# A hybrid decoder step on one core: the opening pipelined by feature tile with products two tiles behind, cache copies moved, the attention's operations reordered

## The chip, the core and the metric

The kernel runs on one core of one Trainium2 chip. Its time is the device time of one execution in microseconds (us); the median of the runs is what is compared. Before the change three runs gave 1983.94, 1985.59 and 1988.86 us, median 1985.59. The core has a matrix engine (TensorE, PE in the profile, with its weight loads apart as PEld), a vector engine (DVE), a scalar engine (ACT), a general engine (GpSimd, POOL) and a queue engine (SyncE, SP), which here issues nearly all transfers. Each engine works through its own instructions in order; semaphores tie them together. All data is float32, and matrix products read it as fp32r, rounded by a cast.

## The reference, cut to what matters

One layer of a decoder trunk for a prompt of 2048 rows and 8 sample rows, of width 1024:

```
mod = c @ w_ada + b_ada;  shift, scale, gate = split(mod, 3)
h = rmsnorm(x, norm_g) * (1 + scale) + shift
z = h @ w_in      # columns: q 1024 | k 256 | v 256 | attention gate | rnn x | rnn gate | merge gates A, B
q, k = rmsnorm per head of 64, times q_g, k_g
o = band_attention(q, k, v)   # blocks of 128 rows over 256 keys, window 128, relative bias, a sink per head
ya = o * silu(ga)
yr = rglru(conv(xr)) * silu(gr)
y = x + gate * ((sigmoid(ma) * (ya @ w_pa) + sigmoid(mr) * (yr @ w_pr)) @ w_out)
```

The sample rows go through the same layer, with their attention over a window of 128 cached rows. The kernel also returns the moved window: rows 1 to 127 of each cache copied down by one row, and a new last row; the same for the convolution's state.

## The kernel before

The prompt is done in two halves of 1024 rows (`s` = 0 and 1). A value that enters a product is held as two fp32r tiles, a high part (an ACT cast) and the rest (a DVE subtraction); a product is three matmuls: high x high, high x low, low x high. This pair of operations is a "split".

**Opening** (lines 1923 to 2103), for the first half. It makes the modulation and h, 128 features (`f`, 8 tiles) at a time, and the k/v products of the first 512 rows on the way, in four PSUM banks `kvp`. For tile f: `mod_load` (286) loads two columns' blocks of `w_ada` (4 transfers of 256 KB); `mod_cols` (309) multiplies them by c on PE (`col_tiled`, 299: products, then an ACT copy of the result) and `mod_finish` (314: two PE transposes, four DVE operations); a DVE operation makes the scale `gsT`; `x_evac(0, f)` (1942) turns four 128x128 blocks of x on PE and `h_evac` (380) applies scale and shift on ACT and splits the result into `hT[f]`; then 24 matmuls multiply it with the k and v weights. From f = 4 on each step also turns two tiles of rows 512 to 1023 (`x_evac(1, ...)`). The x tiles, 128 rows each, are scaled row by row first (`rms_rows`, 365: two squares on ACT, three small operations on POOL, two on DVE). `h_evac` leaves a store of h to DRAM, which runs behind the loop (`late`, 2051). The copies of the caches and of the convolution's state are three DRAM to DRAM transfers issued on POOL's queue (2101 to 2103).

The order of the work is partly the planner's: the framework's scheduler orders instructions by their place in the program and by when it thinks them ready. Instructions issued while `pinned[0]` is set (line 48) keep the order of the program on their engine. In the opening `pinned` is not set; it is set in the attention.

**k/v phase** (`phase_kv`, 506): the remaining rows' k and v, norms, transposes and splits, with the relative bias table on the side. `skn`, the negated sinks, comes from a small load (2060 to 2063).

**Attention** (`phase_attn`, 558): 16 units (4 groups of heads x 4 pairs of row blocks) in a software pipeline over `i`: in one iteration the q product of unit i, the logits and softmax of unit i-1, and the output product of unit i-2. In order: `stage_b4` (softmax normalisation of i-2: DVE reciprocal, POOL multiplication, for each of two row blocks); `gemm_a` (191), the first half of the q product, 24 matmuls into one half of a PSUM bank; `stage_a1` (562) of that half: square on ACT, sum on DVE, power on POOL; `stage_b1`: four transposes of q on PE and its split; the second `gemm_a` into the other half of the same bank and its `stage_a1`; `stage_c1`: eight transposes of the softmax result, a copy on ACT and a masked copy on DVE for each block; `stage_b2`: 24 logit matmuls; `stage_b0`: a small copy on POOL; `stage_c2`: the output product; `stage_b3` of the first block (DVE minimum, ACT exponentials); `stage_a2` (q scaled by its norm on DVE); `stage_c3`; `stage_b3` of the second block. Splits of the next weights are spread over four places of the iteration by `weights` (786), which has due times for each half.

**Recurrent stage and projections** (`stages`, 1254): gates, convolution, recurrence, projections, as steps of 12 matmuls of 512 columns. `line.on(t, rank, fn)` hangs loads, splits and evacuations on step t; weights are loaded 7 steps and split 2 steps ahead.

Of the kernel before, what the change touches and what calls it, by code (L numbers as in the profile page):

```python
# [21 lines left out]
P = 128  # L22
# [19 lines left out]
def tile_hybrid_step(ctx: ExitStack, tc: tile.TileContext, x_prompt, x_sample, cache_k, cache_v, state_conv,  # L42
# [63 lines left out]
    def H(shape, dt=F32):  # L106
        return hp.tile([P] + shape, dt, tag="H", name=nm("H"))
# [73 lines left out]

    def load_half(rows, cols, pin=False):

        return split_raw(load_raw(half_srcs(rows, cols)), 256, pin)
# [373 lines left out]
    def phase_attn(s, hT, sa, kT, vt, chunks, line):  # L558
# [255 lines left out]
        for i in range(N + 2):  # L814
# [25 lines left out]
            if i < N:  # L840
                u, tp = seq[i]
                ps_[i], ss_[i] = PG(), M([8])
                gemm_a(ps_[i], wqs[u], hT, 2 * tp * P, 0)
                stage_a1(ps_[i], ss_[i], 0)
            elif i == N:
                fill(nh - 3)
            else:
                line.emit(0)
            if 1 <= i <= N:
                qk_[i - 1] = stage_b1(ub, tb, qn_.pop(i - 1))  # L850
            weights(2 * i, 1)
            slot(1)
            if i < N:
                if s == 1 and tp == 1:
                    next(smp[u])
                if pend:
                    next(pend.pop(0))
                gemm_a(ps_[i], wqs[u], hT, (2 * tp + 1) * P, 1)
                if pend:
                    next(pend.pop(0))  # L860
                if tp == 3:
                    drop(wqs.pop(u))
                if s == 1 and tp == 1:
                    next(smp[u])
                stage_a1(ps_[i], ss_[i], 1)
            elif i == N:
                fill(nh - 2)
            else:
                line.emit(1)
            weights(2 * i + 1, 0)  # L870
            if 2 <= i:
                t2 = seq[i - 2][1]
                c_[i - 2] = [stage_c1(2 * t2 + t, lt) for t, lt in enumerate(lt_.pop(i - 2))]
                c_[i - 2] = [fn() for fn in c_[i - 2]]
            slot(2)
            if i == N + 1:
                line.emit(2)
            if 1 <= i <= N:
                lps = stage_b2(ub, tb, *qk_.pop(i - 1))
                lts = [stage_b0(ub) for _ in range(2)]  # L880
            if 2 <= i:
                u2, t2 = seq[i - 2]
                po = stage_c2(u2, c_.pop(i - 2))
                if u2 == 3:
                    free(vt[1][t2])
            if 1 <= i <= N:
                sm_[i - 1] = [stage_b3(ub, 2 * tb, lps[0], lts[0])]
# [15 lines left out]
            weights(2 * i + 1, 1)  # L903
# [350 lines left out]
    def stages(s, hT, hT1=None, side=None):  # L1254
# [682 lines left out]

    def kv_load():
        w = w_in[0][len(wkv) * 512:(len(wkv) + 1) * 512]
        wkv.append([load_half(w, [(OFF_K, 256)], True), load_half(w, [(OFF_V, 256)], True)])  # L1940

    def x_evac(g, f):
# [3 lines left out]
        h_evac(0, ps, 512, f, g * 512, hT)  # L1946
        if f == KT - 1:
            free(*xts[4 * g:4 * g + 4])

# [41 lines left out]

    ada_load()
    vrows_first()
# [3 lines left out]
    for xt in xts:  # L1997
        rms_rows([xt[:, 0:512], xt[:, 512:1024]], P)
    ada_load()
    kv_load()  # L2000
    x_load(1)
    ada_load()
    x_load(1)
# [13 lines left out]
    for f in range(KT):  # L2017
        if f < 2:
            ada_load()
            x_load(1)  # L2020
        elif len(ada) < KT:
            if f == 2:
                kv_load()
            ada_load()
        if f < 4:
            xt = xts[4 + f]
            rms_rows([xt[:, 0:512], xt[:, 512:1024]], P)
        if f == 4:
            next(rest)
        if f in (5, 6):  # L2030
            next(table)
        mod_cols([8 + f, f], ada[f], PQ, PT)
        V.tensor_scalar(gsT[:, f, :], modT[:, 8 + f, :], 1.0, VT[:, 24 + f:25 + f], op0=ALU.add, op1=ALU.mult)
        hT.append([S([2, 512], F32R) for _ in range(2)])
        x_evac(0, f)
        xh, xl = col(hT, f, 0, 512)
        for tt in range(4):
# [8 lines left out]
        if f >= 4:  # L2046
            x_evac(1, 2 * (f - 4))
            x_evac(1, 2 * (f - 4) + 1)
    next(rest)
    bias_load()  # L2050
# [49 lines left out]

    for dst, src in ((k_win_s[0, :, 0:127], cache_k[0, :, 1:128]), (v_win_s[0, :, 0:127], cache_v[0, :, 1:128]),
                     (conv_s[0, :, 0:2], state_conv[0, :, 1:3])):
        tc.keep_in_program_order(G_.dma_start(dst, src))
# [41 lines left out]
```

## Time and profile before

| | |
|---|---|
| median of three runs | 1985.59 us (1983.94 to 1988.86) |
| the profiled execution | 1991.77 us, its span 1990.1 us |
| PE busy | 1930.7 us (97%) |
| DVE, ACT, POOL busy | 1375.0, 988.4, 409.4 us |
| mean granted PE clock | 0.995 of full speed |
| moved by DMA | 286.62 MB |

The profile is of one execution. Busy time counts instructions that compute; the ends of matmuls are modelled. A "wait" is idle time of an engine ahead of an instruction and the engine that released it. In the timeline a row is one instruction or several merged ones: start, duration, engine, operation, output and inputs by tile name, shapes, count, and in brackets the idle time before it. The tiles: B and S are the large SBUF buffers, H and M small ones, pg, pq and pt the PSUM banks. Nearly all rows have the line L60, that of the wrapper that issues them, so tile names tell them apart.

### The profile page before, as it was taken

How to read it: one execution, taken by the hardware profiler on the slowest of the kernel's cores; microseconds unless marked ns; L12 is line 12 of the kernel's file. 1: busy time of each engine (PE TensorE's matmuls, PEld its weight loads, DVE VectorE, ACT ScalarE, POOL GpSimd, SP SyncE). 2: the span in 40 equal slices, each digit the busy share in tenths (PEclk: the TensorE clock that was granted, in tenths of full speed). 3: DMA queues.
4: the chain of work that ended last, by engine and by line, in shares of the span. 5: the costliest groups of instructions: out<-in, count | busy, mean ns of one | idle time of the engine just before them, and what ended most of it. 6: DMA issues, size and time to landing. Idle time of an engine off the chain costs nothing. (4 is left out here: it accounts for less than half of the span.)

```text
span 1990.1 us, 32504 instructions
## 1 busy us (share of the span) xinstructions
PE 1930.7 (97%) x11504; PEld 1571.9 (79%) x11504; DVE 1375.0 (69%) x2894; ACT 988.4 (50%) x2199; POOL 409.4 (21%) x540
## 2 busy tenths in 40 slices
PE   6899999999999999999999999999999999999999
PEld 4788887778888878887898888777887877777777
DVE  3447777766878885578744766677677879754965
ACT  4335555435665766514423555543465757542221
POOL 4113443000201112152012344310011111111600
PEclk9999999999999999999999999999999999999999
DMA  9520214552433457986622121445233334458673
GB/s 304 178 75 12 86 49 148 151 183 87 150 98 113 143 180 226 321 296 191 224 60 57 36 62 49 143 130 153 78 118 100 127 102 164 141 174 291 219 230 111
DMA packets 307688, 286.62 MB, mean 144 GB/s; under 512 B 57073, under 2 KB 224229, under 8 KB 307486
## 3 DMA queue, kind: packets, MB, share of 16 engines
q1 hardware_dynamic: 307398, 282.41, 45.3%
q8 instruction: 90, 1.47, 0.3%
q0 software_dynamic: 128, 2.15, 0.3%
q14 instruction: 72, 0.59, 0.1%
HBM read 200.69 MB, written 85.93 MB: 144 GB/s over the span
## 5 line engine op out<-in xcount | busy, mean ns | idle before, releaser
L60 PE MATMUL pg<-S,B 128*128 128x512 f32 (+1 forms) x4224 | 1003.8, 392 | 4.2 <-DVE B L60 3.8
L60 PEld LDWEIGHTS pg<-S,B 128*128 128x128 f32 (+1 forms) x4224 | 773.5, 188 | 189.5 <-issue 11.9
L60 DVE TENSOR_TENSOR B<-B,B 128x512 fp32r<-128x512 f32 (+1 forms) x732 | 537.8, 757 | 157.7 <-ACT B L60 147.9
L60 PE MATMUL pq<-S,B 128*128 128x512 f32 (+2 forms) x1920 | 411.0, 378 | 5.9 <-DVE B L60 5.7
L60 PEld LDWEIGHTS pq<-S,B 128*128 128x128 f32 (+1 forms) x1920 | 316.3, 187 | 84.1 <-DVE B L60 9.7
L60 POOL TENSOR_TENSOR B<-B,B 128x512 f32<-128x512 f32 x128 | 191.3, 1511 | 926.3 <-DVE B L60 518.3
L60 ACT CAST B<-B 128x512 fp32r<-128x512 f32 x468 | 280.3, 617 | 111.2 <-DVE B L60 72.1
L60 PE MATMUL pg<-B,S 128*128 128x256 f32 x1872 | 249.0, 289 | 17.6 <-ACT H L60 12.8
L60 PEld LDWEIGHTS pg<-B,S 128*128 128x128 f32 x1872 | 231.9, 192 | 36.6 <-ACT H L60 19.8
L60 ACT CAST S<-B 128x512 fp32r<-128x512 f32 x184 | 108.8, 620 | 95.8 <-DVE B L60 40.3
L60 DVE TENSOR_TENSOR S<-B,S 128x512 fp32r<-128x512 f32 x184 | 143.2, 808 | 14.8 <-ACT S L60 14.6
L60 ACT ACTIVATE B<-B 128x512 f32<-128x512 f32 (+1 forms) x150 | 93.1, 630 | 116.4 <-DVE B L60 108.7
L60 ACT ACTIVATE B<-B,M 128x129 f32<-128x129 f32 x260 | 102.6, 396 | 72.1 <-DVE M L60 53.4
L60 POOL TENSOR_TENSOR B<-B,M 128x512 f32<-128x512 f32 x64 | 70.4, 1121 | 170.4 <-DVE M L60 170.4
L60 DVE SCALAR_TENSOR_TENSOR B<-B,pg 128x512 f32<-128x512 f32 x78 | 53.1, 682 | 74.8 <-PE pg L60 67.0
L60 POOL TENSOR_TENSOR M<-M,mhalf 128x4 f32<-128x4 f32 (+3 forms) x102 | 96.3, 944 | 8.5
L60 DVE TENSOR_TENSOR B<-pq,B 128x512 f32<-128x512 f32 x96 | 65.9, 686 | 44.1 <-PE pq L60 37.9
L60 ACT COPY B<-pg 128x512 f32<-128x512 f32 x80 | 46.9, 586 | 90.1 <-PE pg L60 81.7
L60 DVE TENSOR_REDUCE M<-H 128x4 f32<-128x256 f32 (+1 forms) x85 | 35.1, 414 | 80.3 <-ACT H L60 79.0
L60 ACT COPY H<-pt 128x256 f32<-128x256 f32 (+1 forms) x47 | 15.6, 333 | 150.1 <-PE pt L60 150.1
L60 DVE SCALAR_TENSOR_TENSOR B<-B,VT,B 128x512 f32<-128x512 f32 x96 | 81.1, 845 | 2.3
L60 DVE SCALAR_TENSOR_TENSOR B<-B,B 128x512 f32<-128x512 f32 x106 | 72.0, 684 | 0.4 <-ACT B L60 0.2
(201 smaller groups left out, 1711.5 us busy)
## 6 DMA issues: line engine op xcount, KB each, us to landing
B<-in_w_in_dram SPq DMA_DIRECT2D x144, 256.0 KB
B<-in_w_in_dram SPq DMA_DIRECT2D x128, 128.0 KB
B<-yad SPq DMA_DIRECT2D x56, 256.0 KB
B<-hd SPq DMA_DIRECT2D x48, 256.0 KB
B<-in_w_out_dram SPq DMA_DIRECT2D x48, 256.0 KB
S<-in_w_ada_dram SPq DMA_DIRECT2D x32, 256.0 KB
S<-in_x_prompt_dram SPq DMA_DIRECT2D x16, 512.0 KB
hd<-B SPq DMA_DIRECT2D x32, 256.0 KB
```

The costliest lines, as they stand in the source:

```text
L60: ins = fn(*args, **kw)
```

## The change

It has four parts, none of which changes what is computed.

- **Opening.** `pinned[0]` is set from the first load to the end of the loop, so that every engine keeps the program's order. The loop runs ten steps in place of eight: step f does the modulation product, the x turns, and the evacuation of tile f, and the k/v products of tile f-2, 12 matmuls before and 12 after `mod_finish`. The k/v weights are loaded early without being split, and split a quarter at a time at even steps (`kv_split`); loads stand in a table by step. The row scalings of x tiles 0 to 3 are in step 0, those of the others in steps 2, 4 and 5. The tiles of rows 512 to 1023 are turned in steps 7 to 9. `bias_load` moves into step 7.
- **Cache copies.** The three transfers leave the opening for steps 46, 60 and 74 of the first half's recurrent stage, still on POOL's queue.
- **q norm.** `stage_a1` squares the whole bank (512 wide) once, after both halves; `stage_a3` sums and takes the power of all 8 columns, behind `stage_c1`'s copies.
- **Order.** Weight splits are done at one place of an iteration, ahead of the second half; `stage_b4` does both blocks in one go; `stage_b0` comes ahead of `stage_c1`'s copies; a slot for steps of the next stage moves behind `stage_c2`.

```diff
-        def stage_a1(ps, ss, t):
-            sq = H([256])
-            A.activation(sq, ps[:, t * 256:(t + 1) * 256], AF.Square)
-            o = ss[:, 4 * t:4 * t + 4]
-            V.tensor_reduce(o, sq.rearrange("p (h d) -> p h d", d=HD), op=ALU.add, axis=AX.X)
-            rstd_of(o, o, 4, 1.0 / HD)
+        def stage_a1(ps):
+            sq = Tt([512])
+            A.activation(sq, ps, AF.Square)
+            return sq
+
+        def stage_a3(sq):
+            ss = M([8])
+            V.tensor_reduce(ss, sq.rearrange("p (h d) -> p h d", d=HD), op=ALU.add, axis=AX.X)
+            free(sq)
+            rstd_of(ss, ss, 8, 1.0 / HD)
+            return ss
...
-                lt_[i - 2] = [stage_b4(*sm_[i - 2][0])]
-            weights(2 * i, 0)
-            if 2 <= i:
-                lt_[i - 2].append(stage_b4(*sm_.pop(i - 2)[1]))
+                lt_[i - 2] = [stage_b4(*x) for x in sm_.pop(i - 2)]
...
                 gemm_a(ps_[i], wqs[u], hT, 2 * tp * P, 0)
-                stage_a1(ps_[i], ss_[i], 0)
...
-            weights(2 * i, 1)
+            weights(2 * i + 1, 1)
             slot(1)
...
-                stage_a1(ps_[i], ss_[i], 1)
+                sq = stage_a1(ps_[i])
...
-            weights(2 * i + 1, 0)
             if 2 <= i:
                 t2 = seq[i - 2][1]
                 c_[i - 2] = [stage_c1(2 * t2 + t, lt) for t, lt in enumerate(lt_.pop(i - 2))]
+            if 1 <= i <= N:
+                lts = [stage_b0(ub) for _ in range(2)]
+            if 2 <= i:
                 c_[i - 2] = [fn() for fn in c_[i - 2]]
-            slot(2)
+            if i < N:
+                ss_[i] = stage_a3(sq)
...
-            weights(2 * i + 1, 1)
...
+            for t, dst, src in ((46, k_win_s[0, :, 0:127], cache_k[0, :, 1:128]),
+                                (60, v_win_s[0, :, 0:127], cache_v[0, :, 1:128]),
+                                (74, conv_s[0, :, 0:2], state_conv[0, :, 1:3])):
+                line.on(t, LOAD, lambda dst=dst, src=src: G_.dma_start(dst, src))
...
+    pinned[0] = True
+    vrows_first()
     ada_load()
...
+    loads = ([lambda: x_load(1), ada_load], [ada_load, kv_load], [lambda: x_load(1), ada_load], [lambda: x_load(2)],
+             [ada_load], [ada_load], [], [], [], [])
...
+    for f in range(KT + 2):
+        for load in loads[f]:
+            load()
+        if f < KT:
+            mn = col_tiled(PT(), cT, ada[f][0], 256)
+            free(*ada[f][1])
+            if f == 0:
+                for i in range(4):
+                    x_rms(i)
+            xps = x_turn(0, f)
+        if f > 1:
+            kv_part(f - 2, (0, 1))
+        if f < KT:
+            mod_finish([8 + f, f], mn, PT)
+            V.tensor_scalar(gsT[:, f, :], modT[:, 8 + f, :], 1.0, VT[:, 24 + f:25 + f], op0=ALU.add, op1=ALU.mult)
+            hT.append([S([2, 512], F32R) for _ in range(2)])
+            x_evac(0, f, xps)
+        if f % 2 == 0 and f < KT:
+            kv_split(f // 4, f % 4 // 2)
+        for i in {7: (0,), 8: (2, 3), 9: (5, 6)}.get(f, ()):
+            second(i)
+        if f > 1:
+            kv_part(f - 2, (2, 3))
+        for i in {2: (4,), 4: (5,), 5: (6, 7)}.get(f, ()):
+            x_rms(i)
...
+        if f == 7:
+            bias_load()
+        for i in {7: (1,), 8: (4,), 9: (7,)}.get(f, ()):
+            second(i)
+    pinned[0] = False
```

More of the change, by code (lines that the diff above doesn't have):

```diff
@@ L879, in phase_attn @@
                 lps = stage_b2(ub, tb, *qk_.pop(i - 1))
-                lts = [stage_b0(ub) for _ in range(2)]
             if 2 <= i:
@@ L885, in phase_attn @@
                     free(vt[1][t2])
+            slot(2)
             if 1 <= i <= N:
@@ L1936, in ada_load, with kv_split, x_turn @@
         ada.append(mod_load([8 + f, f], S, 4))
+    kvr = []
     def kv_load():
-        w = w_in[0][len(wkv) * 512:(len(wkv) + 1) * 512]
-        wkv.append([load_half(w, [(OFF_K, 256)], True), load_half(w, [(OFF_V, 256)], True)])
-    def x_evac(g, f):
+        w = w_in[0][len(kvr) * 512:(len(kvr) + 1) * 512]
+        kvr.append([load_raw(half_srcs(w, [(c, 256)])) for c in (OFF_K, OFF_V)])
+    def kv_split(h, r):
+        if r == 0:
+            wkv.append([[], []])
+        for j in range(2):
+            wkv[h][j].extend(split_raw(kvr[h][j], 256, halves=(r,)))
+    def x_turn(g, f):
         ps = PT() if g else PQ()
@@ L2016, in tile_hybrid_step, with kv_part @@
     rest, table = vrows_rest(), bias_table()
[L2017 to L2035, printed above, removed]
+    def kv_part(f, tts):
         xh, xl = col(hT, f, 0, 512)
-        for tt in range(4):
+        for tt in tts:
             c = slice(tt * P, (tt + 1) * P)
```

30 lines of the change are left out of this document (13 added, 17 removed).

## The prediction, made before the change was run

> **What bounds the kernel now.** I read the page first.
>
> ```profile
> span 1990.1 us, 32504 instructions
> ```
> ```profile
> PE 1930.7 (97%) x11504; PEld 1571.9 (79%) x11504; DVE 1375.0 (69%) x2894; ACT 988.4 (50%) x2199; POOL 409.4 (21%) x540
> ```
>
> TensorE (PE) is the bound: only 1990.1 - 1930.7 = 59.4 us of the span has no matmul running. Work on another engine is worth something only where it makes PE wait or where PE's clock sinks. So the next view is the busy time by stretch, to see where PE is not full.
>
> ```profile
> 0.00:25.00 25.00, 12.33 (x64) 7.16 (x65) 8.24 (x25) 11.97 (x29) 14.07 (x56) 1.00 0.93 284
> 25.00:50.00 25.00, 19.02 (x164) 14.75 (x162) 10.66 (x35) 12.82 (x28) 6.99 (x24) 0.99 1.12 328
> 72.00:76.00 4.00, 4.00 (x21) 4.00 (x21) 0.73 (x5) 0.03 (x1) 0.00 (x0) 0.50 0.46 168
> 116.00:120.00 4.00, 3.24 (x18) 3.25 (x19) 2.17 (x5) 1.33 (x4) 1.20 (x2) 0.71 0.19 73
> 400.00:500.00 100.00, 100.00 (x452) 78.44 (x451) 64.69 (x118) 45.91 (x83) 0.00 (x0) 1.00 0.46 139
> ```
>
> The columns are the stretch, its length, busy time of PE, PE's weight loads, VectorE (DVE), ScalarE (ACT) and GpSimd (POOL), then granted clock, DMA share and GB/s. In the recurrent stages (last row) PE has no gap, so nothing can be won there. In the first 50 us it is busy 31.4 us, while the DMA engines are full (0.93, 1.12): the opening waits for loads. And the clock sinks twice, at 72 and at 116 us. For the rest I asked the waits, first of the matmuls, then of the weight loads.
>
> ```profile
> PE pg L60 <- ACT H L60: 12.8, 19, 1.8
> ```
> ```profile
> PEld pg L60 <- ACT H L60: 19.8, 28, 2.1
> ```
>
> The matmuls' largest wait is for ACT writing an "H" tile: 12.8 us in 19 waits. That tile is the square that `stage_a1` takes of half the q bank. The timeline of one attention iteration shows the mechanism.
>
> ```profile
> 207.01 3.10 PE L60 MATMUL pg<-B,S 128*128 128x256 f32 x24
> 209.95 0.60 PE L60 MATMUL pt<-ident,B 128*128 128x128 f32 x4
> 211.58 3.11 PE L60 MATMUL pg<-B,S 128*128 128x256 f32 x24 [1.04 <-ACT H L60]
> 214.52 1.04 PE L60 MATMUL pt<-ident,B 128*128 128x128 f32 x8
> ...
> 218.98 3.12 PE L60 MATMUL pg<-B,S 128*128 128x256 f32 x24
> ```
> ```profile
> 210.65 0.60 ACT L60 CAST B<-B 128x512 fp32r<-128x512 f32 x1
> 211.16 0.37 ACT L60 ACTIVATE H<-pg 128x256 f32<-128x256 f32 x1
> ```
> ```profile
> 212.21 2.49 POOL L60 TENSOR_TENSOR B<-B,M 128x512 f32<-128x512 f32 x2 [6.05 <-DVE M L60]
> ```
>
> The first half of the q product ends near 209.95. Its square should follow, but ACT still has exponentials and a weight cast (210.65) in its queue and squares only at 211.16. The second half writes the same bank, so PE waits for that read until 211.58. The POOL row is the softmax's normalisation, two tiles of 1.25 us, which the second set of transposes at 214.52 reads.
>
> **The change: attention.** It removes the half squares: `stage_a1` now squares the whole bank behind both halves, so the second half has no reader to wait for. All 28 such waits go. How much is that? Ends of matmuls are modelled; the transposes at 209.95 start about 0.12 us apart, so the next matmul could have started at 210.43, which makes the gap 1.15 us, not the 1.04 shown. The true sum lies between 12.8 (PE) and 19.8 (weight loads, which can stand early for other reasons); with 0.1 us more on most I take **14.5**.
>
> What comes late next? Let an iteration start with the first half at 0. From the starts above a half takes 2.94 us, the four transposes 0.5, the eight 0.97, and the logit and output products together 218.98 - 215.49 = 3.5, where 215.49 is 214.52 plus 0.97; PE alone needs 10.85 us where this iteration took 11.97. The second half ends at 6.4. The square on ACT costs one 512-wide activation (0.63, row below) in place of two 256-wide (0.37 each). `stage_c1`'s transposes end at 7.35, the copy and mask behind them on ACT and DVE at about 8.5, and the output product that reads them starts near 9: 0.5 us of slack. `stage_a3`'s reduction, queued on DVE behind these masks, ends near 9.2, and the power on POOL follows.
>
> ```profile
> L60 POOL TENSOR_TENSOR M<-M,mhalf 128x4 f32<-128x4 f32 x6 | 6.1, 1017 | 0.5
> ```
>
> The power of 8 columns isn't in the trace; it lies between one of 4 (1.02 us) and two (2.03). I take 1.6, nearer to two, since columns and not calls seem to be paid. So `stage_a2` is ready near 11.1 on DVE, just as DVE ends the first softmax part. If the power takes 2.03, the second softmax part behind it on DVE moves by 0.4 us, its exponentials too, and the multiplications on POOL for the next iteration's `stage_c1`. With softmax parts of some 2 us on DVE and 1.25 us for each multiplication, the same walk has those ready near 6.0 and wanted at 6.9; `stage_b4` now issues both reciprocals with no weight split between or ahead of them in its iteration, which helps. So 0.4 us is covered; without this cover it would cost up to 0.4 us in each of 32 iterations, 13 us, the far bound. Weight splits move to one place, between `stage_b1` and the second half; two of them together at three iterations of each sequence half are 1.2 us on ACT, under 2.94 us of matmuls, and cost nothing. I give 1 us back for new waits: **13.5** for this part, bounds 1.5 and 17 (0.15 us under each of the 28 early weight loads left out).
>
> The dip at 116 us follows the first of these waits. With 0.71 granted over 4 us it loses 0.29 x 4 = **1.2 us**, which goes with the wait; at worst nothing.
>
> **The change: opening.** Its rows are a step's modulation, turns and second transposes on PE, the stall, the last product, the loads (count, size), the issue of a small one, and ACT's operations (count, busy us, mean ns).
>
> ```profile
> 37.49 1.07 PE L60 MATMUL pq<-S,cT 128*32 128x256 f32 x16
> 38.49 0.65 PE L60 MATMUL pq<-ident,S 128*128 128x128 f32 x4
> 39.05 0.44 PE L60 MATMUL pt<-ident,H 128*128 128x128 f32 x2
> ```
> ```profile
> 69.23 0.18 DVE L60 TENSOR_SCALAR skn<-M 128x16 f32<-128x16 f32 x1 [5.46 <-DMA M<-in_sinks_dram]
> ```
> ```profile
> 70.65 2.93 PE L60 MATMUL pg<-B,S 128*128 128x256 f32 x12 [3.56 <-DVE S L60]
> ...
> 75.58 0.56 PE L60 MATMUL pq<-B,S 128*128 128x256 f32 x1
> ...
> 77.15 1.90 PE L60 MATMUL pq<-B,S 128*128 128x256 f32 x14
> ...
> 81.00 0.88 PE L60 MATMUL pt<-B,S 128*128 128x256 f32 x6
> ```
> ```profile
> q0 software_dynamic: 128, 2.15, 6.8%
> ...
> S<-in_w_ada_dram SPq DMA_DIRECT2D x32, 256.0 KB
> S<-in_x_prompt_dram SPq DMA_DIRECT2D x8, 512.0 KB
> hd<-B SPq DMA_DIRECT2D x16, 256.0 KB
> B<-in_w_in_dram SPq DMA_DIRECT2D x8, 256.0 KB
> ```
> ```profile
> 53.46 0.41 SPq L60 DMA_DIRECT2D H<-in_b_rg_a_dram  x1
> ```
> ```profile
> L60 ACT ACTIVATE B<-S 128x512 f32<-128x512 f32 x16 | 10.0, 628 | 8.7 <-DMA S<-in_x_prompt_dram 8.5
> L60 ACT CAST S<-B 128x512 fp32r<-128x512 f32 x16 | 9.5, 622 | 0.1
> L60 ACT ACTIVATE B<-pt,modT,gsT 128x512 f32<-128x512 f32 x8 | 6.2, 780 | 12.1 <-PE pt L60 12.1
> ```
>
> Now: the last k/v product of the opening ends at 81.9, with 18 products of the next stage ("pq", from 75.58 to 77.15) already done, 2.2 us at the 2.94/24 = 0.122 of the half above, so the opening is worth 79.7 us. Part of that is the stall at 70.65: DVE's in-order queue held `skn`, which waited for a small load, ahead of the split that PE needed (3.56 us), and the half clock at 72 behind it (0.5 x 4 = 2 us).
>
> After: the loads ahead of the last modulation tile are 8 + 4 + 2 MiB = 14.7 MB. The rows give 25 x 284 = 7.1 MB by 25 us and 328 GB/s from there, so it lands at 25 + 7.6/0.328 = 48.1 us. Before, the copies of the caches (2.15 MB, 6.6 us at that rate) ran in between; the change moves them out. The same sum lands tiles 3, 5 and 6 (7.9, 11.5, 13.6 MB) at 27.4, 38.4 and 44.8.
>
> PE needs per step f: 1.07 modulation, 0.65 turns, 0.44 its transposes, and 24 products of step f-2, 2.9: 5.1 us, less than the 6.5 between landings. But all is in program order now. PE's second transposes wait for ACT's copy (256 wide, as the square at 211.16: 0.37), which stands behind the previous step's evacuation (0.78 + 0.62), weight splits (two casts) and up to two tiles of squares (four of 0.63 and their reads, about 3.3). Walking both queues gives steps 3 to 7 at 28.8, 35.1, 40, 46.4 and 53 us: 5 us behind the loads at the end. From there PE has 1.07 + 0.65 + 0.44, three k/v steps (8.8) and eight turns (5.2), 16.2 us, filled by products two behind: end at 69.2. The gain is 79.7 - 69.2 = **10.5 us**. Bounds: 15.4 if the steps follow the landings (48.1 + 16.2), nothing if ACT's order eats it all.
>
> Moves that cost nothing: POOL's one-hot selections now stand ahead of the first row scaling, in time in which POOL has nothing else until the first x tile has been squared. On SP the nine small vector loads stand ahead of the last modulation load; SP issues ahead of the landings, which hides them, else it is 9 x 0.41 = 3.7 us. The stores of h (4 MiB) follow as a burst and end before the next stage's weights are wanted. The `skn` load is behind the pinned loop now; should its DVE instruction still slip in, 3.56 + 2 us come back. The three copies go on POOL's queue in the recurrent stage, where POOL does nothing (0.00) and the DMA share is 0.46; loads there are issued seven products of 12 matmuls ahead, 84 x 100/452 = 18.6 us, so a copy ahead of one costs nothing, or at worst a few us once.
>
> **Sum.** 10.5 + 13.5 + 1.2 = 25.2 us. The profiled execution took 1991.8 us (span 1990.1 and 1.7 around it), so 1966.6 there. The median of the runs, 1985.59, is 6.2 below it; the prediction is for that median: 1985.6 - 25.2 = **1960.4**.
>
> **The rivals.** (1) The opening pays nothing, because ACT's in-order copies and not the loads set the pace. For it: ACT is the fuller queue of a step with squares. Against: in the first 50 us it is busy 24.8. It leaves 14.7 us of gain: 1970.9. (2) The attention's wait is replaced: the output product waits for its masks, or `stage_c1` for POOL. For it: slacks of 0.5 and 0.9 us only. Against: no engine but PE is full. The opening alone gives 1985.6 - 10.5 - 1.2 = 1973.9. (3) Slower: PE's gaps in the load-bound opening put its clock at half, as after the 3.56 us at 67 us (0.50 at 72). At half clock a step costs 10.2 us, not 5.1: five steps from tile 2 at 24 us end at 75, and the 16.2 become 32.4, together 107, 28 us later than now; less 14.7 it gives 1998.6. It decides once the gap in each step passes about 3.5 us. Against: the first 50 us have 18.6 us of gaps and still a clock of 1.00 and 0.99. (4) No change: the scheduler already hides what is removed, 1985.6.
>
> The Trainium skill ("TensorE: Matmul & The Clock Gate", Part 1) has the rule behind (3): after an idle window of about 3.4 us the array gets half its clock until it has been busy as long. By that rule one long gap costs some 1.7 us and a gap of that length in every step gives rival 3. The trace agrees where PE stood 3.56 us; gaps of 1 to 2 us, which I expect, fall under the window.
>
> **How the numbers follow.** Chances: forecast 0.67, (1) 0.12, (2) 0.13, (3) 0.05, (4) 0.03. Forecast's own best: 15.4 + 17 + 1.2 = 33.6, or 1952; its weak side meets rival 2 at 1974. With a little for the runs' own spread the range is 1951 to 1976; only (3), (4) and part of the tails are outside. A change under 0.3% (6 us) can't be told from none here. Forecast, (1) and (2) are all faster by more: 0.92; same 0.03; slower 0.05.
>
> **What would show it.** Right: no wait of q products for ACT's squares; an iteration near 10.9 us; no DMA on the software queue before 100 us; the eighth modulation product at 49 to 53 us; no stall of PE for DVE near 67; the opening's last k/v product near 68 and the rest shifted by about 25 us. Wrong: waits of "pt" products for DVE or POOL in the attention, a clock near 0.5 over several opening stretches, a modulation product that waits for ACT, or gaps in the recurrent stage near the copies.

## The result, and the profile after

The changed kernel takes 1970.05 us (median of four runs, 1966.61 to 1970.6), the kernel before beside it 1984.94: a ratio of 0.9918, with a 95% interval from 0.9900 to 0.9936, 14.9 us. The prediction was 1960.4 in a range of 1951 to 1976. So the direction and the range were right, and of the 25.2 us that the sum promised 10 did not come. The measured time is the number of the prediction's rival 1 (1970.9), which the range also held. The two terms of the sum were not wrong alike: further down, the attention gives its 14.7 us and more, and the opening next to nothing.

The page of the changed kernel, whose profiled execution took 1970.57 us, and its stretches (the same columns as those shown of before):

```profile
span 1968.9 us, 32371 instructions
...
PE 1918.9 (97%) x11504; PEld 1569.0 (80%) x11504; DVE 1376.8 (70%) x2862; ACT 985.0 (50%) x2167; POOL 391.3 (20%) x476
```
```profile
0.00:25.00 25.00, 10.12 (x65) 4.38 (x67) 7.92 (x28) 9.81 (x23) 12.87 (x64) 1.00 0.93 281
25.00:50.00 25.00, 22.24 (x212) 17.67 (x209) 11.14 (x34) 14.66 (x32) 2.18 (x8) 1.00 0.95 274
72.00:76.00 4.00, 4.00 (x35) 4.00 (x35) 3.12 (x13) 2.12 (x6) 0.20 (x1) 1.00 0.66 225
116.00:120.00 4.00, 4.00 (x19) 3.25 (x18) 1.85 (x4) 0.60 (x1) 2.12 (x4) 1.00 0.00 0
```

Both sinks of the clock that the prediction named (0.50 at 72 us, 0.71 at 116) are gone, but the clock sinks at other places in this trace:

```profile
52.00:56.00 4.00, 2.46 (x12) 2.49 (x13) 1.96 (x8) 0.71 (x1) 0.29 (x1) 0.69 1.03 350
84.00:88.00 4.00, 3.37 (x16) 2.86 (x15) 2.90 (x15) 1.77 (x5) 0.90 (x3) 0.53 0.00 0
```

The clock is still 0.88 and 0.62 in the 4 us behind each; by the granted shares these four stretches lose 5.1 us. The stretches from 48 to 56 us had lost 1.7 us in the trace of before, those from 84 to 92 us nothing.

PE did less in the first 25 us than before (10.12 against 12.33) and more in the next 25 (22.24 against 19.02): by 50 us the rebuilt opening has gained 1 us of matmul time. The waits of the matmuls:

```profile
PE pt L60 <- DMA S<-in_w_ada_dram: 6.7, 6, 2.3
...
PE pt L60 <- POOL B L60: 5.8, 6, 1.5
...
PE pt L60 <- DVE H L60: 3.2, 1, 3.2
PE pt L60 <- DVE RT L60: 3.1, 1, 3.1
```

The line of 12.8 us, the waits of "pg" products for ACT's "H", is no longer there. Four have grown or are new: modulation products that wait for their weights (1.7 us before, under the tile name "pq"), output transposes that wait for POOL (1.4 us before, in five waits of at most 0.3), one wait of transposes for a small DVE copy ("H"), and one for the copy of the recurrent state ("RT"). An attention iteration of the first half, in the timeline of the changed kernel:

```profile
178.14 3.09 PE L60 MATMUL pg<-B,S 128*128 128x256 f32 x24
181.07 1.04 PE L60 MATMUL pt<-ident,B 128*128 128x128 f32 x8
...
188.80 3.09 PE L60 MATMUL pg<-B,S 128*128 128x256 f32 x24
```

From one second half of the q product to the next it is 188.80 - 178.14 = 10.66 us, with no idle time in brackets, where the iteration of before took 11.97.

To see where the time went I took the start of each instruction of PE, DVE and ACT in two traces, paired the n-th of each form (operation, tiles, shape) with the n-th of the other trace, and took the median difference in a stretch: the lead. The kernel before was traced a second time for this (below); its second trace spans 1983.2 us and its execution took 1984.9, where the first took 1991.8. The leads in us, by the time in the trace of before:

```
lead over the kernel before       100-110  120-130  310-400  900-1000  1290-1400  1900-
changed kernel, over trace 1          4.6      8.3     20.8      20.7       20.4   21.3
changed kernel, over trace 2         -1.4      2.3     14.9      14.4       14.1   14.4
opening alone, over trace 2          -1.3      0.2     -0.3      -1.9       -2.0   -2.7
old opening, skn late, trace 2        1.2      2.7      2.8       2.7        2.7    2.6
changed + samples' power, trace 2     1.9      5.6      18.2     17.5       25.7   23.5
all three repairs, trace 2            5.5      8.4      21.0     20.5       30.5   27.6
```

The second row ends nearest to the gain between the medians (14.4 against 14.9), though each row compares one execution with one other. In it the opening and the k/v phase leave the changed kernel 1.4 us behind at 100 us, the first wait of the attention gives 3.7, the rest of the first half's attention 12.6 (14.9 - 2.3), and the second half nothing more (14.4 to 14.1 across its attention).

### The profile page after: what moved, and what is told of

Same layout as the page of the kernel before. It is cut to its first block, busy times and chain, and to the rows that moved or that the text cites. A ratio compares the mean times of both kernels' runs of the same rounds, so it can differ in the third digit from the quotient of the medians.

```text
span 1968.9 us, 32371 instructions
## 1 busy us (share of the span) xinstructions
PE 1918.9 (97%) x11504; PEld 1569.0 (80%) x11504; DVE 1376.8 (70%) x2862; ACT 985.0 (50%) x2167; POOL 391.3 (20%) x476
## 3 DMA queue, kind: packets, MB, share of 16 engines
q8 instruction: 90, 1.47, 0.3%
## 5 line engine op out<-in xcount | busy, mean ns | idle before, releaser
L60 PE MATMUL pg<-B,S 128*128 128x256 f32 x1872 | 243.3, 286 | 0.0
L60 DVE TENSOR_TENSOR S<-B,S 128x512 fp32r<-128x512 f32 x184 | 144.6, 814 | 25.9 <-ACT S L60 25.7
L60 ACT ACTIVATE B<-pg 128x512 f32<-128x512 f32 x76 | 45.2, 595 | 85.3 <-PE pg L60 85.3
L60 POOL TENSOR_TENSOR M<-M,mhalf 128x8 f32<-128x8 f32 (+4 forms) x70 | 83.8, 1198 | 5.8
L60 DVE TENSOR_TENSOR B<-pt,mcT 128x512 f32<-128x512 f32 x64 | 41.7, 686 | 47.4 <-ACT B L60 45.5
```

The source lines that it names most:

```text
L60: ins = fn(*args, **kw)
```

## The experiments

Every kernel is compared with runs of the kernel before on the same chip, by ratio; 1% is 19.9 us.

**The attention part alone.** The kernel before with the functions and the loop of the attention replaced by the new ones.

> The kernel before with the attention part of the change alone (one square over both halves of the q product, the new order of the operations); opening and cache copies as before. My theory: the part is worth its full 13.5 us in the first half of the sequence only, and in the second half what it wins is given back by the output transposes that wait for POOL's normalisation behind the samples' small power. So about 12 us under the kernel before, 1973, with a wait of pt products for POOL of 5 to 6 us in the second half. Rival one, the prediction as it stands: 13.5 + 1.2 us, 1970, no POOL wait. Rival two, the whole gain of the change (14.9 us between the medians) comes from this part: 1970 and the opening alone gives nothing.

Measured: 1972.61 us against 1989.05, ratio 0.9911 (0.9891 to 0.9932), 17.7 us. The wait for POOL is there, in the waits of this kernel:

```profile
PE pt L60 <- POOL B L60: 5.9, 6, 1.5
```

So the attention alone gives as much as the whole change. The interval, 13.5 to 21.7 us, leaves out the 12 us of my theory and holds the 14.7 and 14.9 of the rivals. In this trace the second half's attention gains 2.8 us by the leads, where the changed kernel's gains nothing: the waits for POOL are the same, but no low clock stands behind them. What they cost is tested below.

**The opening and the copies alone.** The changed kernel with the old attention put back.

> The changed kernel with the attention of before: opening and cache copies of the change alone. My theory: the opening's last k/v product ends some 8.7 us earlier than before, and about 4 us of it are lost again in the k/v phase, where PE waits for DVE's copy of the recurrent state: 3 to 5 us under the kernel before, 1981. Rival one, the prediction: 10.5 us, 1974.5. Rival two: nothing, 1985.

Measured: 1987.67 against 1989.05, ratio 0.9993 (0.9983 to 1.0002). Nothing that can be told from no change, at most 3.4 us: my theory of 3 to 5 us fell by the median, and rival two held. What the theory had been built on was the lead over the first trace of before.

**The kernel before, traced again.**

> The kernel before once more, for a second trace. Its first trace, on which the prediction's sum was made, took 1991.8 us where the median of its runs is 1985. My theory: the order of DVE's queue is the same, so PE stands for skn again, by 2.9 to 3.6 us (the kernel with the old opening and the new attention showed 2.9), and what differs between executions is the granted clock behind such waits: a lead or lag of 2 to 5 us by 130 us. Rival: the stall comes from a late landing of the sinks in that one execution and is under 1 us here, which would take most of the opening's gain away from the typical run.

Measured: 1984.9 us. The rival held. In the first trace DVE waited 5.46 us at skn for the sinks; in the second, the rows of DVE, PE, SP and the stretch at 72 us:

```profile
65.79 0.17 DVE L60 TENSOR_SCALAR skn<-M 128x16 f32<-128x16 f32 x1 [1.63 <-DMA M<-in_sinks_dram]
```
```profile
67.32 1.58 PE L60 MATMUL pg<-B,S 128*128 128x256 f32 x12
...
75.06 0.86 PE L60 MATMUL pt<-B,S 128*128 128x256 f32 x6
```
```profile
63.08 0.41 SPq L60 DMA_DIRECT2D M<-in_sinks_dram  x1
```
```profile
72.00:76.00 4.00, 4.00 (x36) 3.99 (x35) 3.12 (x10) 2.88 (x8) 0.00 (x0) 1.00 0.67 231
```

and SP's row for the same load in the first trace:

```profile
64.96 0.40 SPq L60 DMA_DIRECT2D M<-in_sinks_dram  x1
```

SP issued the load 1.9 us later in the first trace, and it took 3.9 us from the end of the issue to skn's start, against 2.3 in the second. The wait of 1.63 us on DVE is covered: the 12 products that waited 3.56 us in the first trace (70.65) start here at 67.32 without a bracket. The clock at 72 us is 1.00, not 0.50. From there the second trace is 6.0 us ahead of the first. The stall is thus no fixed part of the program. Of the three traces with the old opening's order, two show it (3.56 us in the first trace, 2.92 in the kernel with the new attention alone) and one doesn't. How often it comes is not known: on the chip of the second trace the median of the kernel before is 1987.72 us, so the execution without the stall, at 1984.9, is one of the quicker ones there.

**The old opening without the stall.** The kernel before, with the lines of `sk` and `skn` moved behind `phase_kv`.

```diff
-    sk = M([NH])
-    ld.dma_start(sk, sinks[0].partition_broadcast(P))
...
+    sk = M([NH])
+    ld.dma_start(sk, sinks[0].partition_broadcast(P))
...
     attn.send(pend)
```

> The kernel before with the load of the sinks and the DVE instruction that makes skn behind the k/v phase, nothing else. In the traces the changed opening is no earlier than the old one up to 60 us and 5.6 us earlier at 70 us, where the old one stands still for skn. My theory: nearly all that the changed opening wins is this stall, 3.6 us and the low clock behind it, so this one move is worth 3 to 6 us on the kernel before, as much as the rebuilt opening or more. Rival: the stall is made good in the k/v phase by the norms of the k tiles, which would hold PE up in any case: under 1.5 us.

Measured: 1984.53 against 1987.89, ratio 0.9984 (0.9975 to 0.9993), 3.2 us. The interval is 1.4 to 5.0 us. My theory held by the median: a move of one small operation is worth as much as the rebuilt opening, in which the same operation also stands elsewhere. A stall of some 6 us in part of the executions could give a median gain of this size, but that the 3.2 us are the stall alone is not shown: this kernel's trace also leads the second trace of before, which has no stall, by 2.7 us, of which 1.2 are there ahead of skn and 1.5 come at 112 us, where the clock of that trace sinks to 0.64.

**The copies back in the opening.** The first try put the three transfers behind `x_rms(5)` in step 4.

> The changed kernel with the three copies of caches and state issued on POOL in step 4 of the opening, near 44 us, where the kernel before issued them, and not in the recurrent stage. My theory: from step 6 on PE's own chain and SP's late issue set the pace and the DMA engines are at 0.60 to 0.68 there, so the copies cost 0 to 2 us: 1970 to 1972. Rival, the prediction's sum: the loads set the pace and 2.15 MB of copies push them by 6.6 us: 1976.5.

Measured: 1979.5 against 1989.05, ratio 0.9950 (0.9932 to 0.9968), some 6.5 us over the changed kernel, just the rival's number, but not for its reason. The DVE row:

```profile
62.14 0.18 DVE L60 TENSOR_SCALAR skn<-M 128x16 f32<-128x16 f32 x1 [13.09 <-DMA M<-in_sinks_dram]
```

The scheduler had moved the unpinned skn ahead of the pinned row scalings of step 5, and DVE stood 13 us for a load that SP issues behind all the others. So this run told nothing of the copies, and much of what one unpinned operation can do. The second try keeps skn in program order.

```diff
-    V.tensor_scalar(skn.rearrange(
+    tc.keep_in_program_order(V.tensor_scalar(skn.rearrange(
```

> The changed kernel with the three copies issued in step 4 of the opening again, this time with skn kept behind the opening in DVE's queue; in the earlier kernel with the copies in step 4, skn had come ahead of the row scalings of step 5 and held DVE for 13 us, so it told nothing of the copies. My theory: the DMA engines have room near 44 to 52 us (0.60 to 0.68 busy) and step 7 waits for PE's own stall anyway: 0 to 2 us over the changed kernel. Rival, the prediction's sum: 2.15 MB ahead of the last modulation load cost 6.6 us.

Measured: 1967.97 against 1987.72, ratio 0.9900 (0.9883 to 0.9917); the changed kernel has 0.9918 and 0.9913. No cost shows in the medians (it is even 3 us under, within the intervals), as my theory had it, and the prediction's 6.6 us fell. The stretches from 44 to 52 us of the changed kernel, then of this one:

```profile
44.00:48.00 4.00, 3.08 (x34) 2.15 (x33) 1.68 (x7) 1.26 (x2) 0.74 (x2) 1.00 0.68 170
48.00:52.00 4.00, 2.31 (x24) 1.88 (x16) 1.57 (x3) 3.08 (x10) 1.80 (x6) 1.00 0.60 173
```
```profile
44.00:48.00 4.00, 2.71 (x26) 1.98 (x24) 2.00 (x8) 1.60 (x3) 2.27 (x4) 1.00 1.20 362
48.00:52.00 4.00, 2.66 (x24) 2.04 (x24) 1.40 (x3) 2.74 (x9) 2.12 (x6) 1.00 0.85 310
```

The DMA share (second number from the right) shows why so little is at stake: where the copies ran, the changed kernel leaves a third of the DMA engines' time unused, since SP spends 41.6 to 48.1 us on nine small loads before it issues the last modulation load. The copies are not quite free, though. With them SP's issue of that load ends at 54.8 us, not at 50.3, and the products of step 7 wait for it:

```profile
56.56 0.64 PE L60 MATMUL pt<-S,cT 128*32 128x256 f32 x8 [1.18 <-DMA S<-in_w_ada_dram]
58.86 0.72 PE L60 MATMUL pt<-S,cT 128*32 128x256 f32 x8 [1.67 <-DMA S<-in_w_ada_dram]
```

The last product of the opening starts at 73.24 us against 70.40 in the changed kernel. By the leads the trace is 2.2 us behind the changed kernel's first at 60 to 70 us and 1.0 from 100 us to the end of the first half's attention; it makes that good in the second half's attention, where its clock doesn't sink. The two traces of the changed kernel differ by 1.9 us at 100 us, so 1 us is no more than executions differ by.

**The samples' power.** In the changed kernel one step of `stage_s`, the square, sum and power of the samples' q, stands at the end of an iteration, so ahead of the next iteration's normalisation on DVE and POOL. Here it is moved behind `stage_a3`.

```diff
                 ss_[i] = stage_a3(sq)
+                if s == 1 and tp == 1:
+                    next(smp[u])
...
-            if s == 1 and i < N and tp > 0:
+            if s == 1 and i < N and tp > 1:
                 next(smp[u])
```

> The changed kernel with one step of the samples' q norm (square on ACT, sum on DVE, power of 8x4 on POOL) moved from the end of an iteration, where it stands ahead of the next iteration's normalisation on DVE and POOL, to just behind the sum and power of the q product. Three iterations of the second half are touched. My theory: POOL's normalisation starts 1.5 to 2 us earlier there, the 5.8 us in which pt products wait for POOL go, and with them two dips of the clock (0.66, 0.91 and 0.64, 0.94 over 4 us each, together 3.4 us): about 9 us under the changed kernel, 1961. Rival one: the normalisation is late because POOL's multiplications run beside DVE's weight splits (two took 3.02 us there and 2.04 elsewhere), so most of the wait stays: 1967. Rival two: the next wait takes its place at once (ACT's square or the masks), nothing: 1970.

Measured: 1961.95 against 1989.05, ratio 0.9865 (0.9847 to 0.9883), some 10.7 us under the changed kernel. My theory held. The rows of POOL, DVE and PE in the changed kernel, and the clock behind them:

```profile
1119.81 0.19 POOL L60 TENSOR_SCALAR M<-M 8x4 f32<-8x4 f32 x1 [4.28 <-DVE M L60]
1120.08 1.00 POOL L60 TENSOR_TENSOR M<-M,mhalf 8x4 f32<-8x4 f32 x1
1120.55 2.63 DVE L60 TENSOR_TENSOR B<-B,B 128x512 fp32r<-128x512 f32 x2
1121.06 3.02 POOL L60 TENSOR_TENSOR B<-B,M 128x512 f32<-128x512 f32 x2
1122.69 0.66 PE L60 MATMUL pt<-ident,B 128*128 128x128 f32 x4 [1.47 <-POOL B L60]
...
1124.13 0.66 PE L60 MATMUL pt<-ident,B 128*128 128x128 f32 x4 [0.79 <-POOL B L60]
```
```profile
1124.00:1128.00 4.00, 3.87 (x32) 3.12 (x34) 3.21 (x9) 1.03 (x4) 1.44 (x5) 0.66 0.12 36
1128.00:1132.00 4.00, 4.00 (x32) 3.14 (x29) 3.81 (x19) 3.43 (x17) 0.74 (x1) 0.91 0.82 255
```

The tiny power (8 by 4 values) takes 1.00 us of POOL just ahead of the two multiplications, these run beside two weight splits on DVE, and PE stands 1.47 and 0.79 us. In the moved version the power runs early and the normalisation starts at once:

```profile
1112.51 0.19 POOL L60 TENSOR_SCALAR M<-M 8x4 f32<-8x4 f32 x1
1112.79 1.00 POOL L60 TENSOR_TENSOR M<-M,mhalf 8x4 f32<-8x4 f32 x1
1116.26 2.04 POOL L60 TENSOR_TENSOR B<-B,M 128x512 f32<-128x512 f32 x2 [2.48 <-DVE M L60]
```
```profile
1100.00:1125.00 25.00, 25.00 (x232) 22.70 (x231) 20.83 (x73) 15.42 (x55) 10.86 (x14) 1.00 0.31 95
1125.00:1150.00 25.00, 25.00 (x234) 22.71 (x233) 18.27 (x69) 16.34 (x59) 10.99 (x16) 1.00 0.03 13
```

PE is full and its clock whole where the changed kernel had its gaps; by the leads the second half's attention gives 8.2 us (17.5 to 25.7).

**The changed kernel, traced again.**

> The changed kernel once more, with a second trace. It tells how far one execution's opening stands for all. In the trace of the sample-power kernel, whose opening has the same instructions, the opening ran 1.9 to 3.3 us shorter than in the first trace of the changed kernel. My theory: the 3.2 us wait of PE for DVE's copy at step 6 and the 3.1 us wait in the k/v phase come back in each execution, since they come from the order of the queues, and only the granted clock behind them differs: 1.5 to 3.5 us between two traces. Rival: the waits themselves are accidents of one execution and are not there this time.

Measured: 1968.53 us median against 1987.89, ratio 0.9913 (0.9895 to 0.9931). All three waits are there again: 3.34 us at step 6 for "H", 3.12 in the k/v phase for "RT", 5.8 in all for POOL. My theory held for the waits. For the clock it was too narrow: this trace (span 1975.9, clock 0.990) is 7 us behind the first, 1.9 of them by 100 us, 2.9 in the second half's attention, and 3 behind 1300 us, where none of the three waits stands.

**Two operations of the opening.** The table's copy ahead of the row scalings of step 5; the small vector loads one step later.

```diff
+        if f == 5:
+            next(table)
         for i in {2: (4,), 4: (5,), 5: (6, 7)}.get(f, ()):
             x_rms(i)
-        if f == 4:
+        if f == 5:
             next(rest)
-        if f in (5, 6):
+        if f == 6:
             next(table)
```

> The changed kernel with two operations of the opening in another place: the copy of the one-hot table ahead of the row scalings of step 5, so that DVE's queue doesn't hold the bank that PE's transposes of step 6 want, and the nine small vector loads behind the last modulation load, not ahead of it. My theory: the wait of 3.2 us at step 6 goes, with the low clock behind it (0.69 and 0.88 over 4 us each, 1.7 us), and step 7 starts near 51 to 53 and not 57: 4 to 6 us under the changed kernel. Rival: the landings set the pace of steps 6 and 7 anyway, so PE waits for the last modulation load in place of DVE: under 1.5 us.

Measured: 1967.12 against 1987.89, ratio 0.9889 (0.9875 to 0.9903), 4.8 us less than the changed kernel in the same set. My theory held by the median, though the intervals of the two overlap; step 7 starts at 54.69 us, not at 51 to 53. First the stall in the changed kernel, DVE and PE, then step 7 in this one:

```profile
52.33 0.88 DVE L60 TENSOR_SCALAR S<-S,M 128x512 f32<-128x512 f32 x2 [0.71 <-POOL M L60]
53.13 0.27 DVE L60 COPY H<-pt 32x128 f32<-32x128 f32 x1
...
53.54 0.66 PE L60 MATMUL pt<-ident,H 128*128 128x128 f32 x2 [3.24 <-DVE H L60]
...
57.11 1.07 PE L60 MATMUL pt<-S,cT 128*32 128x256 f32 x16
```
```profile
54.69 1.07 PE L60 MATMUL pt<-S,cT 128*32 128x256 f32 x16
...
83.56 0.69 PE L60 MATMUL pt<-ident,H 128*128 128x128 f32 x2 [2.83 <-ACT S L60]
```

The copy of the one-hot table waits in DVE's queue behind row scalings, which wait for POOL's power, and holds a PSUM bank that PE's transposes of step 6 want. Without that, step 7 starts 2.4 us sooner. But the last row shows that the k/v phase has its own wait, now under the name of ACT.

**The recurrent state later.** The loads, turns and copy of `RT` behind `phase_kv`.

> The changed kernel with the loads, the eight turns and the copy of the recurrent state (tile RT) behind the k/v phase in the program, not ahead of it. My theory: the 3.1 us in which PE waits for DVE's copy of RT go, and with them the clock of 0.53 and 0.62 over the next 8 us (3.4 us): 4 to 6 us under the changed kernel. Rival: PE would have run out of work there anyway, because the norms of the four k tiles that the opening ends with all at once go one after the other, 2.4 us each through ACT, DVE and POOL, and hold the banks: the wait gets another name and stays, under 1.5 us.

Measured: 1969.0 against 1987.89, ratio 0.9904 (0.9890 to 0.9918), 1.8 us less than the changed kernel, within the intervals. Neither side holds outright; the rival comes nearer. The one wait of 3.13 us

```profile
83.13 0.44 PE L60 MATMUL pt<-ident,H 128*128 128x128 f32 x2 [3.13 <-DVE RT L60]
```

in the changed kernel becomes four smaller ones here:

```profile
78.62 0.44 PE L60 MATMUL pt<-ident,H 128*128 128x128 f32 x2 [1.35 <-DVE H L60]
...
80.95 0.41 PE L60 MATMUL pt<-ident,H 128*128 128x128 f32 x2 [0.94 <-DVE M L60]
...
84.05 0.44 PE L60 MATMUL pt<-ident,H 128*128 128x128 f32 x2 [0.56 <-DVE S L60]
...
86.18 1.12 PE L60 MATMUL pt<-S,B 128*128 128x512 f32 x2 [0.74 <-ACT S L60]
```

3.6 us in sum, which fits the rival: four k tiles end together with the opening, and their norms go one behind the other through ACT, DVE and POOL. But the clock, 0.53 and 0.62 behind the one long wait, stays at 1.00 from 76 to 100 us here, and by the leads this trace is 2.3 us ahead of the changed kernel's first at 100 us.

**Old opening or new.** Last, two best versions. One has the old opening with skn late, the new attention and the samples' power moved:

> The kernel before with the new attention, the samples' power behind the q product's, and the sinks' load and skn behind the k/v phase: the old opening without its one stall. The three were measured apart as 17.7, 10.8 and 3.2 us; together 31.7, so 1956 on a chip where the kernel before takes 1988. My theory: the rebuilt opening is worth no more than the skn move, so this is 4 to 6 us under the changed kernel with the sample power moved (ratio 0.9865, 1961). Rival: the rebuilt opening is worth 3 us or more in the typical run and this comes out at 1960 or above.

Measured: 1959.96 against 1987.72, ratio 0.9863 (0.9842 to 0.9884). The changed kernel with the power moved alone has 0.9865. So the rebuilt opening is worth no more than the move of skn, to within the intervals of some 4 us, but the 4 to 6 us by which I thought the old one better are not there: the time is the rival's 1960.

The other is the changed kernel with the three repairs:

> The changed kernel with all three repairs: the samples' power behind the q product's, the table's copy and the small loads in the other place, the recurrent state behind the k/v phase. By the single runs 17.3 + 10.8 + 4.8 + 1.8 = 34.7 us under the kernel before, ratio 0.9826, 1953 on a chip where that takes 1988. My theory: the sample power adds in full, the two repairs of the opening overlap by 1 to 2 us, since an earlier end of the opening meets the same chain of k norms: 1953 to 1956. Rival: the k norms take back all that the two repairs give, 1960.

Measured: 1957.16 against 1987.72, ratio 0.9842 (0.9825 to 0.9860), 31 us under the kernel before and some 14 under the changed one, whose interval lies apart. This beats both kernels. It misses the expected 1953 to 1956 by 1 us, less than its interval, so no overlap of the repairs beyond the 1 to 2 us assumed is shown. Against the old opening's version it gains 2.8 us in the medians, within the intervals.

## Why the prediction was right, and where it was wrong

The forecast was 25.2 us and 14.9 came. The number is rival 1's: the opening paid next to nothing. That the time still lies in the range owes something to the range, which held rival 1, and something to luck in the attention.

**Attention, 13.5 us and 1.2 for the clock: right in mechanism for the first half; near in size by two errors that offset each other.** The part alone measured 17.7 us. No q product waits for a square, an iteration of the first half takes 10.66 us (10.85 was given for PE alone), and POOL's power of 8 columns took 1.64 us where 1.6 was assumed. The walk through the slack was right too for an iteration with only the prompt's work in it. What it left out was the samples' work in the second half. `stage_s` was in the code and its 8x4 power in the trace of before; I walked one iteration of the first half and multiplied by 32. So rival 2 held in three iterations of the second half: 5.8 us of waits and the clock behind them, 10.7 us by the run that removes them. The forecast asked what is late next, and asked it of the wrong half. So new waits, put at 1 us, cost some 8 to 11. What hid this is that the gain was low by about as much: by the leads the first half alone gives 3.7 + 12.6 = 16.3 us and the second, once the power is moved, 8.2, some 24.5 where 14.5 + 1.2 stood. Why the part gives more than the brackets of the old waits sum to is not shown; the new order of the operations came with it.

**Opening, 10.5 us: wrong; it is worth 1.4 us at most likely, and by its interval (0.9983 to 1.0002) between a gain of 3.4 and a loss of 0.4.** Three steps failed.

First, the base. "Part of that is the stall at 70.65 ... (3.56 us), and the half clock at 72 behind it (0.5 x 4 = 2 us)": 5.6 of the 10.5 us were this stall, and it belongs to some executions only. The text noted that the profiled execution lay 6.2 us above the median and took the sum off the median all the same. The second trace has no stall and is 6.0 us ahead from 70 us on, about what the first lay above its median. Out of a median, moving skn takes 3.2 us (1.4 to 5.0) and not 5.6; and since the rebuilt opening, which holds this move too, gives 1.4, nothing that can be told is left for the rest of it. Taken off the profiled execution, as the rest of the sum was, the forecast would have been 1966.6.

Second, the walk. "steps 3 to 7 at 28.8, 35.1, 40, 46.4 and 53 us" held within 0.9 us up to 46.4 (PE's products of step 6 start at 46.31) and missed the last by 4 us, 57.11. It had followed PE and ACT, but not DVE, on which the table's copy stands behind the row scalings. Against the old opening little was gained by then: the lead at 60 to 70 us is 1.7 us over the second trace. Rival 1 was the right one, with another engine in the leading part.

Third, the end.

```profile
70.40 0.87 PE L60 MATMUL pt<-B,S 128*128 128x256 f32 x6
```

The opening's last product ends at 70.40 + 0.87 = 71.27 us, not 69.2, or 71.0 less two products done ahead; in the second trace of before it ends at 75.06 + 0.86 = 75.92, less the same 2.2 us of products done ahead 73.7. So 2.7 us were left. The k/v phase behind then took them, and more (-1.4 at 100 us): the forecast treated the end of the opening as the start of everything behind it. What stood there was the wait of 3.13 us for RT and the clock of 0.53 and 0.62 behind it. That four k tiles which end together meet one chain of norms fits the waits of the two runs that changed this place, but no run takes the chain apart.

**The copies: the 6.6 us of DMA time were real, and worth 1 us behind the k/v phase in one trace and nothing that the medians show.** In the changed kernel the landing of the last modulation load was set by SP's queue: its issue ends at 50.3 us. The sentence that SP "issues ahead of the landings, which hides them, else it is 9 x 0.41 = 3.7 us" had the right alternative at hand; 41.6 to 48.1 us is what it came to. In the recurrent stage the copies cost nothing that shows in the leads (14.9 to 14.4 us over 600 us).

**The other expectations.** Step 7 at 49 to 53 and the last product near 68 were missed; the shift of the rest was 21 us against the first trace, 14 against the second. Rivals 3 and 4 did not come. Why the timed gain of the attention alone (17.7) exceeds that of the whole change (14.9 and 17.3 in two sets) stays within the intervals, and open.

## What to carry to other kernels

When the profiled execution lies above the median, look for the stall that makes the difference before pricing anything: a wait that ends with a small load's landing is the first suspect, and its price in one trace is not its price in the median. In a software pipeline walk the iteration with the most side work, not the typical one: there something tiny ahead of the critical operation in an in-order queue stops the bound engine. And where a scheduler may place an unpinned operation among pinned ones, look where it put it: skn alone moved the time by 3 us in one place and by some 10 in another.

## What the runs showed of the hardware

**The clock after short gaps.** The prediction took gaps of 1 to 2 us in the opening as free of any loss of clock, although its own sum had 1.2 us for the dip behind one of 1.84 us. They are not free, and not regularly so. The wait of 1.84 us at the first attention unit was followed by a clock of 0.71 in the first trace of before, one of 1.88 by 0.64 in the second; the same wait in the kernel with the new opening alone, and in the old opening without the stall, was not: 24 products in 3.10 us,

```profile
112.07 3.10 PE L60 MATMUL pg<-B,S 128*128 128x256 f32 x24 [1.87 <-ACT H L60]
```

where the same 24 took 4.64 in both traces of before. The POOL waits of 1.47 and 0.79 us cost the clock of 0.66 and 0.91 shown above, while the same pair in the kernel with the new attention alone (1.52 and 0.79) cost none:

```profile
1124.00:1128.00 4.00, 1.69 (x13) 1.25 (x13) 3.19 (x4) 1.83 (x4) 4.00 (x5) 1.00 0.97 314
1128.00:1132.00 4.00, 4.00 (x45) 2.88 (x45) 3.17 (x10) 1.27 (x4) 1.43 (x3) 1.00 0.23 67
```

The two traces of the changed kernel, which is one program, differ too: at 1670 us a wait of 1.60 us left the clock at 1.00 and ten products took 2.60 us; in the other trace a wait of 1.82 us at the same place was followed by 0.62, and the ten took 3.79. So in these traces a gap of 1.5 to 2 us has a price of 0 to 2 us beside its own length, and the same place of one program can pay it in one execution and not in another. The Trainium skill ("TensorE: Matmul & The Clock Gate", Part 1) says that the window of about 3.4 us runs freely; that fits a dip that comes in one execution and not in the next. Its limit of one idle window is longer than these gaps, and here the measurement decides.

**POOL and DVE side by side.** Two 128x512 multiplications on POOL took 2.04 us in the changed kernel where DVE had no work beside them,

```profile
139.55 2.04 POOL L60 TENSOR_TENSOR B<-B,M 128x512 f32<-128x512 f32 x2 [5.64 <-DVE M L60]
```

and 3.02 where two weight splits on DVE had begun 0.51 us ahead of them. The splits took 2.63 us there against 1.29 for two elsewhere in the changed kernel:

```profile
57.36 1.29 DVE L60 TENSOR_TENSOR B<-B,B 128x512 fp32r<-128x512 f32 x2
```

In the version with the power moved POOL began first, by 1.1 us: its pair took 2.04 us, as without company, and the splits 2.10.

The Trainium skill ("GPSIMD Engine Reference", 8. Key points) names it: POOL shares its ways into SBUF with DVE, and operations of DVE with two SBUF inputs contend. The trace agrees.
